# Router work laid along the slabs of the last attention projection, and memory's first steps behind the first experts

## The chip, the core and the metric

The kernel runs on one core of a Trainium2 chip. A core has engines with queues of their own: TensorE (PE in the profile, with its weight loads as PEld), VectorE (DVE), ScalarE (ACT), GpSimd (POOL) and SyncE (SP), which here issues the loads from HBM. Weights come into on-chip memory (SBUF) by DMA; products land in PSUM, in eight banks. The metric is the device time of one execution in microseconds (us), the median of several runs. Every fp32 weight is split into a high and a low part (h and l), and each product of a projection is three matmuls: h by xh, l by xh, h by xl.

## What is computed

A small decoder with two parts, for 256 tokens of width 1024, in fp32. Block 1 is attention and a mixture of 32 experts in four groups, with two experts for each token; behind it come two more layers (mixers, cross-attention into 256 memory tokens, a feed-forward part). Cut to what the change touches:

```python
x = x + mixed @ w_out[l]
x = x + hierarchical_moe(rmsnorm(x, ffn_norm[l]), ...)

def hierarchical_moe(h, ...):
    g_logits = hf @ w_rg + b_rg                # 4 groups
    g_sel = argmax(g_logits)
    p_group = softmax(g_logits)[g_sel]
    e_logits = einsum('td,gde->tge', hf, w_re) + b_re
    top_vals, top_idx = top_k(e_logits[g_sel], 2)
    weight = p_group * softmax(top_vals)
    ...
    ys = (silu(xb @ w_g[e]) * (xb @ w_u[e])) @ w_d[e]
    out = out.at[slot_tok].add(ys * slot_w)

def mem_attention(h, mem_n, ...):              # both later layers
    kv = (mem_n @ w_kv)                        # depends on mem alone
```

The keys and values of the memory depend on no token, so the kernel may compute them anywhere ahead of the later layers.

## The kernel before, in words

**Recording and planning.** The program is first recorded by `Recorder` (line 161) as a list of operations, then put in order by `plan` (line 290), a list scheduler with a price for each operation: each engine takes, of what is ready, the operation with the lowest place in the recording (`bias` shifts that place). It also hands out buffers. A tile has a tag; tiles of one tag take their slots in the order of recording. Loads are handed their slots strictly in that order too. A raw expert load (`raw`, line 542) has no tag: it takes a slot of whichever shared tag has most to spare, counting as taken those that tiles recorded ahead of it will still need (`spare`, line 309). Shared are `n8` (6 slots), `w`, `h` and `l` (3 each); each slot holds 1 MiB. The framework then fixes the final order of the single instructions on each engine, which may let one with a free slot pass another that waits.

**Slabs.** `slab` (line 548) loads 1 MiB of weights into `w`, ACT copies it into `h`, DVE subtracts into `l`. `fm` (line 672) multiplies a slab by all 256 tokens, channel by channel, into a PSUM bank of tag `g` (three banks).

**The last projection.** `block1_attention` (line 794) ends with one memory step (`prepare`, line 1325: load of the memory, its scaled parts and statistics) and `project` (line 711): four slabs of w_out, each followed by an add into x.

**The router.** `moe` (line 1046) then transposes x into the tiles hh and hl (16 transposes of 128 by 128), takes the squares of x (`sumsq`, line 653), and calls `route` (line 957): products with the router's weights `wr` as the stationary operand (36 columns, 256 tokens moving), a copy, two transposes back, some forty short DVE instructions that select groups and experts, a prefix count on PE (`pos`), and place. Two memory steps (`values`, line 1353) are recorded behind that with a lower priority (`MEM_EARLY`, `FILL`).

**The experts.** `gather` (line 1097) makes the selection matrix st for eight experts, picks their tokens by 32 matmuls, and makes each slot's norm factor and expert weight by matmuls of two scaled copies (rt, ct) with a column of ones (`rs`). Eight groups of four experts follow: `gate_up` (line 1142, eight raw loads of w_gu), `gated` (line 1154), `expert_out` (line 1168, four raw loads of w_dn). Between them stand memory steps, as many as `MEM_EVERY` says (line 36). Of 18 memory steps 16 are done by the end of the experts; the last two go into the following mixer.

Of the kernel before, what the change touches and what calls it, by code (L numbers as in the profile page):

```python
# [10 lines left out]
F32 = mybir.dt.float32  # L11
# [20 lines left out]
CUT = 2  # L32
MEM_EARLY = 2
FILL = 300
LATEG = 1
MEM_EVERY = (2, 2, 2, 2, 2, 2, 1, 0)

# [15 lines left out]
for _name, _width in (("ident", 128), ("cmask", 128), ("smask", 128), ("ulow", 128), ("ntri", 128),  # L53
                      ("bd64", 128), ("dist", 256), ("cm", 32), ("sm", 32), ("cb", 16), ("sb", 16),
                      ("slot", 32)):
    CST[_name] = (_off, _off + _width)
    _off += _width
# [104 lines left out]
class Recorder:  # L162
    LAG = 200.0
    shared = ("n8", "w", "h", "l")
    OWN = 70.0
# [306 lines left out]
class Net:  # L472
# [237 lines left out]

    def project(self, w, m):

        for s in range(4):
            b = self.fm(self.slab(w[s], 256), m)
            xs = self.x[:, 2 * s:2 * s + 2, :]
            self.rec.vector.tensor_tensor(xs, xs, self.two(b), ALU.add)


# [74 lines left out]

    def block1_attention(self, steps):
        nc, a = self.rec, self.a
# [127 lines left out]
        for n, wn in enumerate(("w_o_mla", "w_o_moba")):  # L923
            for s in range(2):
                w = self.slab(a[wn][s], 512)
                for q in range(2):
# [4 lines left out]
                    if n:  # L931
                        m = gates[0][:, c:c + 2, :]
                        nc.vector.tensor_tensor(m, m, gv, ALU.add)
                        self.parts(mx[0][:, c:c + 2, :], mx[1][:, c:c + 2, :], m)
        steps.pop(0)()
        self.project(a["w_out"], mx)

# [18 lines left out]

    def route(self, rtm):

        nc = self.rec
        tt, ts, red = nc.vector.tensor_tensor, nc.vector.tensor_scalar, nc.vector.tensor_reduce  # L960
        wr = self.temp("a", "wr", [128, KC, 36])
        tt(wr, self.par("wr").rearrange("p (k n) -> p k n", n=36),
           self.par("ffn_norm")[:, :, None].to_broadcast([128, KC, 36]), ALU.mult)
        b = self.bank("a", "rt")
        for k in range(KC):
            self.mm(b[0:36, :T], wr[:, k, :], self.x[:, k, :], k == 0, k == KC - 1)
        lt = self.temp("a", "lt", [128, T])
        nc.vector.tensor_copy(lt[0:36, :], b[0:36, :T])
        b = self.bank("a", "rt2")
        for t in range(2):  # L970
            nc.tensor.transpose(b[:, 64 * t:64 * t + 36], lt[0:36, 128 * t:128 * t + 128], self.ident[0:36, 0:36])
        board, used = self.temp("a", "route", [128, 400]), [0]

        def small(name, *s):
            if name in ("wt", "place", "wlate"):
                return self.small(name, 2, *s, bufs=1)
            o, used[0] = used[0], used[0] + 2 * int(np.prod(s))
            v = board[:, o:used[0]]
            return v.rearrange({0: "p t -> p t", 1: "p (t a) -> p t a", 2: "p (t a b) -> p t a b"}[len(s)],
                               **({"t": 2, "a": s[0]} if s else {}))  # L980
# [21 lines left out]
        tt(oa, o1, o2, ALU.add)  # L1002
        sel, wt = small("sel", 4, 8), small("wt", 4, 8)
        grouped = lambda out, v: [tt(out[:, t], v[:, t, None, :].to_broadcast([128, 4, 8]),
                                     g1[:, t, :, None].to_broadcast([128, 4, 8]), ALU.mult) for t in range(2)]
        grouped(sel, oa)
        sel, wtf = (q.rearrange("p t g e -> p t (g e)") for q in (sel, wt))
        selb = self.small("selb", 2, 32, dt=BF16, bufs=1)
# [34 lines left out]
        nc.vector.tensor_copy(flag[0:1, :], b[0:1, 0:1])  # L1043
        return wtf, place, wlate, flag

    def moe(self, steps, early, every):
# [3 lines left out]
        for q in range(2):  # L1050
            for t in range(2):
                b = self.bank("g", "xt")
                for j in range(4):
                    nc.tensor.transpose(b[:, 128 * j:128 * j + 128], x[:, 4 * q + j, 128 * t:128 * t + 128],
                                        self.ident)
                cs = slice(512 * q, 512 * q + 512)
                self.parts(hh[:, t, cs], hl[:, t, cs], b)
        rtm = self.rstd_by_token(self.sumsq(x))
        wt, place, wlate, flag = self.route(rtm)
        nc.bias = -FILL  # L1060
        for _ in range(early):
            steps.pop(0)()
        nc.bias = 0
        self.next = []
        xs, rest = self.gather(0, hh, hl, place, wt, rtm)
        banks = [self.bank("a", "gu")]
        self.gate_up(0, range(KC), xs, banks[0])
        for g in range(8):

            (st, rw), q = rest, g % 2  # L1070
# [8 lines left out]
            self.expert_out(g, 0, at, st, rw, q)  # L1079
            take = every[g]  # L1080
            if take:
                steps.pop(0)()
            if g < 7:
                self.gate_up(g + 1, range(KC // 2, KC), ahead, banks[g + 1])
            self.expert_out(g, 1, at, st, rw, q)
            if g % 2 == 0 and g < 6:
                ahead, later = self.gather(g // 2 + 1, hh, hl, place, wt, rtm)
            if q:
                xs = ahead
                if g < 7:  # L1090
                    rest = later
            if g == LATEG:
                nc.barrier(lambda: self.moe_late(hh, hl, rtm, wlate, flag), [hh, hl, rtm, wlate, flag, x])
            for _ in range(max(0, take - 1)):
                steps.pop(0)()

    def gather(self, p, hh, hl, place, wt, rtm):

        nc, slot = self.rec, self.c("slot")
        st = self.temp("a", "st", [128, 2, 8, SLOTS], F32R)  # L1100
        ct, rt = (self.temp("b", n, [128, 2, 8, SLOTS]) for n in ("ct", "rt"))
        for t in range(2):
            pe = lambda v: v[:, t, 8 * p:8 * p + 8][:, :, None].to_broadcast([128, 8, SLOTS])
            nc.vector.tensor_tensor(st[:, t], pe(place), slot[:, None, :].to_broadcast([128, 8, SLOTS]),
                                    ALU.is_equal)
            nc.vector.tensor_scalar(rt[:, t], st[:, t], rtm[:, t:t + 1], None, ALU.mult)
            nc.vector.tensor_tensor(ct[:, t], st[:, t], pe(wt), ALU.mult)
        stv, ctv, rtv = (v.rearrange("p t e s -> p t (e s)") for v in (st, ct, rt))
        xs = self.big("xs", [128, KC, 256])
        for i in range(4):  # L1110
# [6 lines left out]
            for j in range(2):  # L1117
                c = 2 * i + j
                gc = self.gcol("ffn_norm", c)
                if j:  # L1120
                    nc.scalar.activation(xs[:, c, :], b[:, 256 * j:256 * j + 256], AF.Copy, scale=gc)
                else:
                    nc.vector.tensor_scalar(xs[:, c, :], b[:, 256 * j:256 * j + 256], gc, None, ALU.mult)
        b = self.bank("m", "rs")
        for n, v in enumerate((rtv, ctv)):
            for i in range(2):
                for t in range(2):
                    self.mm(b[:, 2 * n + i:2 * n + i + 1], v[:, t, 128 * i:128 * i + 128], self.kone,
                            t == 0, t == 1)
        rw = self.small("rw", 4)  # L1130
        nc.vector.tensor_copy(rw, b[:, :4])

        b = self.bank("m", "sb")
        for i in range(2):
            for t in range(2):
                o = 256 * i + 128 * t
                nc.tensor.transpose(b[:, o:o + 128], stv[:, t, 128 * i:128 * i + 128].step("bitcast", F32), self.ident)
        sb = self.small("sb", 2, T, dt=F32R)
        nc.vector.tensor_copy(sb, self.two(b))
        return xs, (sb, rw)  # L1140

# [475 lines left out]
    def record(self, out):  # L1617
        steps = self.memory()
        self.block1_attention(steps)
        self.moe(steps, MEM_EARLY, MEM_EVERY)  # L1620
        x, rbc = self.two_norms()
# [94 lines left out]
def shape_constants():  # L1716
    c = np.zeros((128, NCST), np.float32)

    def put(name, v):
        s, e = CST[name]  # L1720
        c[:, s:e] = np.asarray(v, np.float32).reshape(128, e - s)
# [10 lines left out]
    for cn, sn, half in (("cm", "sm", 16), ("cb", "sb", 8)):  # L1732
# [3 lines left out]
        for n, fn in ((cn, np.cos), (sn, np.sin)):  # L1736
            put(n, fn(ang.astype(np.float64)).reshape(2, 128, half).transpose(1, 0, 2))
    put("slot", np.broadcast_to(np.arange(SLOTS) - 999.0, (128, SLOTS)))
    return c
# [16 lines left out]
```

## Time and profile before

| | us |
|---|---|
| median of 3 runs | 1278.55 |
| lowest and highest | 1278.52, 1281.36 |
| profiled execution, its own time | 1273.56 |
| its span, first to last instruction | 1271.8 |
| mean granted TensorE clock | 0.985 |

The busy shares on the page are means over the whole span; the two lines of digits below show how DMA traffic (GB/s) and PE move through it, in 40 slices of 31.8 us.

```profile
PE   7999999997889877997999999999999999999998
GB/s 274 237 100 133 205 249 210 323 411 356 420 419 419 419 383 290 186 147 100 169 163 67 216 194 184 172 197 172 160 133 133 118 165 100 182 197 173 185 177 64
```

Block 1's attention fills the first six slices, the router lies in the seventh, and the experts with most of the memory steps in slices 8 to 16.

### The profile page before, as it was taken

How to read it: one execution, taken by the hardware profiler on the slowest of the kernel's cores; microseconds unless marked ns; L12 is line 12 of the kernel's file. 1: busy time of each engine (PE TensorE's matmuls, PEld its weight loads, DVE VectorE, ACT ScalarE, POOL GpSimd, SP SyncE). 2: the span in 40 equal slices, each digit the busy share in tenths (PEclk: the TensorE clock that was granted, in tenths of full speed). 3: DMA queues.
4: the chain of work that ended last, by engine and by line, in shares of the span. 5: the costliest groups of instructions: out<-in, count | busy, mean ns of one | idle time of the engine just before them, and what ended most of it. 6: DMA issues, size and time to landing. Idle time of an engine off the chain costs nothing.

```text
span 1271.8 us, 22754 instructions
## 1 busy us (share of the span) xinstructions
PE 1213.5 (95%) x9371; PEld 1084.3 (85%) x9371; DVE 861.4 (68%) x1546; ACT 648.0 (51%) x1103; POOL 9.0 (1%) x70
## 2 busy tenths in 40 slices
PE   7999999997889877997999999999999999999998
PEld 7999999674555644997999999999999999999997
DVE  7666677424462345997787977777755687877775
ACT  7664554223332235555554655455766655555543
POOL 1000000000000000000000000000000000000000
PEclk9999999999899999998999999999999999999999
DMA  7623565898999997542541655555433342555551
GB/s 274 237 100 133 205 249 210 323 411 356 420 419 419 419 383 290 186 147 100 169 163 67 216 194 184 172 197 172 160 133 133 118 165 100 182 197 173 185 177 64
DMA packets 40141, 273.53 MB, mean 215 GB/s; under 512 B 4576, under 2 KB 4576, under 8 KB 8032
## 3 DMA queue, kind: packets, MB, share of 16 engines
q1 hardware_dynamic: 40032, 272.03, 57.2%
q8 instruction: 74, 1.21, 0.4%
q14 instruction: 35, 0.29, 0.1%
HBM read 270.96 MB, written 1.05 MB: 214 GB/s over the span
## 4 chain that ended last, share of the span: by engine, by line
PE 67%; DVE 5%; DMA 2%; ACT 1%; issue 0%; SPq 0%; ACTq 0%
PE fm L469 42%; PE dn L469 10%; PE tm L469 4%; PE gu L469 2%; PE oz L469 1%; DVE l L469 1%; PE mo L469 1%; PE ms L469 1%; DMA w<-w_gu 1%; PE by L469 1%; DMA w<-w_xkv 1%; PE hn L469 1%; DVE x L469 1%; PE bo L469 1%; PE st L469 1%; PE ga L469 0%
## 5 line engine op out<-in xcount | busy, mean ns | idle before, releaser
L469 PE MATMUL fm<-xh,h 128*128 128x256 f32 x1824 | 528.1, 290 | 17.1 <-ACT h L469 9.6
L469 PE MATMUL fm<-xh,l 128*128 128x256 f32 x1824 | 520.4, 286 | 5.8 <-DVE l L469 5.8
L469 PE MATMUL fm<-xl,h 128*128 128x256 f32 x1824 | 519.4, 285 | 0.0
L469 DVE TENSOR_TENSOR l<-w,h 128x1024 fp32r<-128x1024 f32 (+2 forms) x328 | 383.3, 1191 | 60.8 <-ACT h L469 60.0
L469 ACT ACTIVATE h<-w 128x1024 fp32r<-128x1024 f32 (+2 forms) x328 | 326.0, 1027 | 173.2 <-issue 84.3
L469 PEld LDWEIGHTS fm<-xh,h 128*128 128x128 f32 x1824 | 351.8, 193 | 26.3 <-ACT h L469 11.0
L469 PEld LDWEIGHTS fm<-xh,l 128*128 128x128 f32 x1824 | 352.0, 193 | 8.1 <-DVE l L469 7.5
L469 PEld LDWEIGHTS fm<-xl,h 128*128 128x128 f32 x1824 | 351.8, 193 | 6.0 <-issue 4.7
L469 PE MATMUL tm<-h,xh 128*128 128x256 f32 (+2 forms) x364 | 108.8, 300 | 0.9 <-DVE x L469 0.6
L469 PE MATMUL tm<-l,xh 128*128 128x256 f32 (+2 forms) x364 | 105.2, 290 | 3.1 <-DVE l L469 3.1
L469 PE MATMUL tm<-h,xl 128*128 128x256 f32 (+2 forms) x364 | 104.9, 289 | 0.0
L469 PEld LDWEIGHTS tm<-h,xh 128*128 128x128 f32 x364 | 70.5, 194 | 6.8 <-issue 3.6
L469 PEld LDWEIGHTS tm<-l,xh 128*128 128x128 f32 x364 | 70.6, 194 | 4.5 <-DVE l L469 3.7
L469 DVE SCALAR_TENSOR_TENSOR fc<-fu,partile,fc 128x256 f32<-128x256 f32 x176 | 73.5, 479 | 1.3 <-ACT fc L469 1.3
L469 PEld LDWEIGHTS tm<-h,xl 128*128 128x128 f32 x364 | 70.5, 194 | 2.8 <-issue 2.5
L469 PE MATMUL gu<-w,xs 128*32 128x512 f32 x512 | 67.3, 633 | 0.2 <-PEq L1206 0.2
L469 PE MATMUL dn<-fa,h 128*128 128x256 f32 x352 | 64.2, 282 | 1.1 <-ACT fa L469 0.6
L469 PE MATMUL dn<-h,fa 128*128 128x512 f32 x176 | 57.0, 396 | 0.0
L469 DVE TENSOR_TENSOR fu<-fm,rbc 128x512 f32<-128x512 f32 x44 | 30.3, 688 | 37.9 <-PE fm L469 37.7
L469 PEld LDWEIGHTS dn<-fa,h 128*128 128x128 f32 x352 | 54.4, 189 | 1.6 <-ACT fa L469 0.8
L469 DVE SCALAR_TENSOR_TENSOR yl<-by,rw,yh 128x512 fp32r<-128x512 f32 x16 | 12.0, 749 | 55.7 <-ACT yh L469 55.7
L469 PE MATMUL dn<-fa,l 128*128 128x256 f32 x176 | 49.6, 282 | 0.0
(276 smaller groups left out, 1375.2 us busy)
## 6 DMA issues: line engine op xcount, KB each, us to landing
w<-w_gu SPq DMA_DIRECT2D x64, 1024.0 KB, 10.9
w<-w_up SPq DMA_DIRECT2D x44, 1024.0 KB, 4.9
w<-w_dn SPq DMA_DIRECT2D x32, 1024.0 KB, 12.4
w<-w_down SPq DMA_DIRECT2D x22, 1024.0 KB, 4.9
w<-w_xkv SPq DMA_DIRECT2D x16, 1024.0 KB, 9.2
w<-w_in_d SPq DMA_DIRECT2D x8, 1024.0 KB, 4.8
w<-w_xq SPq DMA_DIRECT2D x8, 1024.0 KB, 4.9
w<-w_xo SPq DMA_DIRECT2D x8, 1024.0 KB, 4.9
```

Of the source, the lines that this page charges most:

```text
L469: self.last[engine.engine] = getattr(engine, method)(*map(r, a), **{n: r(v) for n, v in k.items()})
```

## The change

Each slab of w_out is followed at once by its share of what the router needs. `project` gets a function `after` that runs behind each slab's add: two chunks of x times `wr` for both halves of the tokens (x is now the stationary operand, so the logits come out by token and the copy and the two transposes back are gone), the squares of the two chunks, and behind every second slab the transposes and the split into hh and hl.

No memory step is recorded ahead of the experts any more: `prepare` leaves `block1_attention`, `MEM_EARLY` and `FILL` are gone, and `MEM_EVERY` is larger (16 steps instead of 13), the first three of them at the end of group 0. The tags `xh` and `xl` join the shared ones, each with two slots.

`gather` is split. The part that picks tokens stays; the factors are made in `scatter`, recorded for the first pair of groups behind `gate_up(0)`: the transposed selection times one matrix `factors` of 33 columns (the norm factor and 32 expert weights), of which each slot takes its own column with a constant mask `own`.

```diff
-MEM_EARLY = 2
-FILL = 300
-MEM_EVERY = (2, 2, 2, 2, 2, 2, 1, 0)
+MEM_EVERY = (3, 2, 2, 3, 2, 2, 2, 0)
...
-    shared = ("n8", "w", "h", "l")
+    shared = ("n8", "w", "h", "l", "xh", "xl")
...
-    def project(self, w, m):
+    def project(self, w, m, after=None):
...
             self.rec.vector.tensor_tensor(xs, xs, self.two(b), ALU.add)
+            if after:
+                after(s)
...
-        steps.pop(0)()
-        self.project(a["w_out"], mx)
+        return mx
...
-        for k in range(KC):
-            self.mm(b[0:36, :T], wr[:, k, :], self.x[:, k, :], k == 0, k == KC - 1)
-        lt = self.temp("a", "lt", [128, T])
-        nc.vector.tensor_copy(lt[0:36, :], b[0:36, :T])
-        b = self.bank("a", "rt2")
-        for t in range(2):
-            nc.tensor.transpose(b[:, 64 * t:64 * t + 36], lt[0:36, 128 * t:128 * t + 128], self.ident[0:36, 0:36])
...
+        def prepared(s):
+
+            for k in (2 * s, 2 * s + 1):
+                for t in range(2):
+                    self.mm(logits[:, 64 * t:64 * t + 36], x[:, k, 128 * t:128 * t + 128], wr[:, k, :],
+                            k == 0 and t == 0, k == KC - 1)
+            self.squares(self.pair(x, s), acc, s == 0)
+            if s % 2:
+                q = s // 2
+                for t in range(2):
+                    b = self.bank("g", "xt")
+                    for j in range(4):
+                        nc.tensor.transpose(b[:, 128 * j:128 * j + 128], x[:, 4 * q + j, 128 * t:128 * t + 128],
+                                            self.ident)
+                    cs = slice(512 * q, 512 * q + 512)
+                    self.parts(hh[:, t, cs], hl[:, t, cs], b)
+
+        self.project(a["w_out"], mx, prepared)
+        rtm = self.rstd_by_token(acc)
+        factors, place, wlate, flag = self.route(rtm, logits)
...
-        rtm = self.rstd_by_token(self.sumsq(x))
-        wt, place, wlate, flag = self.route(rtm)
-        nc.bias = -FILL
-        for _ in range(early):
-            steps.pop(0)()
-        nc.bias = 0
...
+        xs, st = self.gather(0, hh, hl, place)
         banks = [self.bank("a", "gu")]
         self.gate_up(0, range(KC), xs, banks[0])
+        rest = self.scatter(0, st, factors)
...
-            if take:
+            if g and take:
                 steps.pop(0)()
...
-            for _ in range(max(0, take - 1)):
+            for _ in range(take if g == 0 else max(0, take - 1)):
...
-            nc.vector.tensor_scalar(rt[:, t], st[:, t], rtm[:, t:t + 1], None, ALU.mult)
-            nc.vector.tensor_tensor(ct[:, t], st[:, t], pe(wt), ALU.mult)
...
+    def scatter(self, p, stv, factors):
+        one = lambda t, i: stv[:, t, 128 * i:128 * i + 128].step("bitcast", F32)
+        b = self.bank("m", "rs")
+        for i in range(2):
+            for t in range(2):
+                self.mm(b[:, 64 * i:64 * i + 33], one(t, i), factors[:, t, :], t == 0, t == 1)
+        bv = b[:, :128].rearrange("p (i n) -> p i n", i=2)
...
+        nc.vector.tensor_copy(rw[:, 0:2], bv[:, :, 0])
+        nc.vector.tensor_tensor(own, bv[:, :, 1 + 8 * p:9 + 8 * p],
+                                self.c("own").rearrange("p (i e) -> p i e", i=2), ALU.mult)
+        nc.vector.tensor_reduce(rw[:, 2:4], own, axis=AX.X, op=ALU.add)
```

More of the change, by code (lines that the diff above doesn't have):

```diff
@@ L54 @@
                       ("bd64", 128), ("dist", 256), ("cm", 32), ("sm", 32), ("cb", 16), ("sb", 16),
-                      ("slot", 32)):
+                      ("slot", 32), ("own", 16)):
     CST[_name] = (_off, _off + _width)
@@ L791, in rope, with block1_attention @@
         tt(x2, ts[2], ts[3], ALU.add)
-    def block1_attention(self, steps):
+    def block1_attention(self):
         nc, a = self.rec, self.a
@@ L955, in first_of, with route @@
         nc.vector.tensor_tensor(out, order, m[:, :, None].to_broadcast(shape), ALU.is_equal)
-    def route(self, rtm):
+    def route(self, rtm, b):
         nc = self.rec
         tt, ts, red = nc.vector.tensor_tensor, nc.vector.tensor_scalar, nc.vector.tensor_reduce
[L961 to L964, printed above, removed]
-        for k in range(KC):
-            self.mm(b[0:36, :T], wr[:, k, :], self.x[:, k, :], k == 0, k == KC - 1)
-        lt = self.temp("a", "lt", [128, T])
-        nc.vector.tensor_copy(lt[0:36, :], b[0:36, :T])
-        b = self.bank("a", "rt2")
-        for t in range(2):
-            nc.tensor.transpose(b[:, 64 * t:64 * t + 36], lt[0:36, 128 * t:128 * t + 128], self.ident[0:36, 0:36])
         board, used = self.temp("a", "route", [128, 400]), [0]
         def small(name, *s):
-            if name in ("wt", "place", "wlate"):
+            if name in ("place", "wlate"):
                 return self.small(name, 2, *s, bufs=1)
@@ L1002, in route @@
         tt(oa, o1, o2, ALU.add)
-        sel, wt = small("sel", 4, 8), small("wt", 4, 8)
+        sel = small("sel", 4, 8)
+        factors = self.small("factors", 2, 33, bufs=1)
+        nc.vector.tensor_copy(factors[:, :, 0], rtm)
+        wtf = factors[:, :, 1:33]
+        wt = wtf.rearrange("p t (g e) -> p t g e", g=4)
         grouped = lambda out, v: [tt(out[:, t], v[:, t, None, :].to_broadcast([128, 4, 8]),
@@ L1006, in route @@
         grouped(sel, oa)
-        sel, wtf = (q.rearrange("p t g e -> p t (g e)") for q in (sel, wt))
+        sel = sel.rearrange("p t g e -> p t (g e)")
         selb = self.small("selb", 2, 32, dt=BF16, bufs=1)
@@ L1043, in route, with moe @@
         nc.vector.tensor_copy(flag[0:1, :], b[0:1, 0:1])
-        return wtf, place, wlate, flag
-    def moe(self, steps, early, every):
+        return factors, place, wlate, flag
+    def moe(self, steps, every, mx):
         nc, a, x = self.rec, self.a, self.x
         hh, hl = (t.rearrange("p (t q) n -> p t (q n)", t=2) for t in self.xtiles())
[L1050 to L1057, printed above, removed]
-        rtm = self.rstd_by_token(self.sumsq(x))
-        wt, place, wlate, flag = self.route(rtm)
-        nc.bias = -FILL
-        for _ in range(early):
-            steps.pop(0)()
-        nc.bias = 0
+        acc = self.tile([128, 512], "acc", "acc", 2)
+        wr = self.temp("a", "wr", [128, KC, 36])
+        nc.vector.tensor_tensor(wr, self.par("wr").rearrange("p (k n) -> p k n", n=36),
+                                self.par("ffn_norm")[:, :, None].to_broadcast([128, KC, 36]), ALU.mult)
+        logits = self.bank("a", "rt")
+        def prepared(s):
[16 more added lines that the diff above has]
+        factors, place, wlate, flag = self.route(rtm, logits)
@@ L1064, in moe @@
         self.next = []
-        xs, rest = self.gather(0, hh, hl, place, wt, rtm)
+        xs, st = self.gather(0, hh, hl, place)
         banks = [self.bank("a", "gu")]
         self.gate_up(0, range(KC), xs, banks[0])
+        rest = self.scatter(0, st, factors)
         for g in range(8):
-            (st, rw), q = rest, g % 2
+            (sb, rw), q = rest, g % 2
             at = self.gated(banks[g], rw, q)
@@ L1078, in moe @@
                 self.next.append(self.slab(a["w_eqk"][0], 256))
-            self.expert_out(g, 0, at, st, rw, q)
+            self.expert_out(g, 0, at, sb, rw, q)
             take = every[g]
-            if take:
+            if g and take:
                 steps.pop(0)()
@@ L1084, in moe @@
                 self.gate_up(g + 1, range(KC // 2, KC), ahead, banks[g + 1])
-            self.expert_out(g, 1, at, st, rw, q)
+            self.expert_out(g, 1, at, sb, rw, q)
             if g % 2 == 0 and g < 6:
-                ahead, later = self.gather(g // 2 + 1, hh, hl, place, wt, rtm)
+                ahead, st = self.gather(g // 2 + 1, hh, hl, place)
+                later = self.scatter(g // 2 + 1, st, factors)
             if q:
@@ L1093, in moe, with gather @@
                 nc.barrier(lambda: self.moe_late(hh, hl, rtm, wlate, flag), [hh, hl, rtm, wlate, flag, x])
-            for _ in range(max(0, take - 1)):
+            for _ in range(take if g == 0 else max(0, take - 1)):
                 steps.pop(0)()
-    def gather(self, p, hh, hl, place, wt, rtm):
+    def gather(self, p, hh, hl, place):
         nc, slot = self.rec, self.c("slot")
         st = self.temp("a", "st", [128, 2, 8, SLOTS], F32R)
-        ct, rt = (self.temp("b", n, [128, 2, 8, SLOTS]) for n in ("ct", "rt"))
         for t in range(2):
-            pe = lambda v: v[:, t, 8 * p:8 * p + 8][:, :, None].to_broadcast([128, 8, SLOTS])
-            nc.vector.tensor_tensor(st[:, t], pe(place), slot[:, None, :].to_broadcast([128, 8, SLOTS]),
-                                    ALU.is_equal)
-            nc.vector.tensor_scalar(rt[:, t], st[:, t], rtm[:, t:t + 1], None, ALU.mult)
-            nc.vector.tensor_tensor(ct[:, t], st[:, t], pe(wt), ALU.mult)
-        stv, ctv, rtv = (v.rearrange("p t e s -> p t (e s)") for v in (st, ct, rt))
+            pe = place[:, t, 8 * p:8 * p + 8][:, :, None].to_broadcast([128, 8, SLOTS])
+            nc.vector.tensor_tensor(st[:, t], pe, slot[:, None, :].to_broadcast([128, 8, SLOTS]), ALU.is_equal)
+        stv = st.rearrange("p t e s -> p t (e s)")
         xs = self.big("xs", [128, KC, 256])
@@ L1123, in gather @@
                     nc.vector.tensor_scalar(xs[:, c, :], b[:, 256 * j:256 * j + 256], gc, None, ALU.mult)
+        return xs, stv
+    def scatter(self, p, stv, factors):
+        nc = self.rec
+        one = lambda t, i: stv[:, t, 128 * i:128 * i + 128].step("bitcast", F32)
         b = self.bank("m", "rs")
[L1125 to L1129, printed above, removed]
-        rw = self.small("rw", 4)
-        nc.vector.tensor_copy(rw, b[:, :4])
+        for i in range(2):
+            for t in range(2):
+                self.mm(b[:, 64 * i:64 * i + 33], one(t, i), factors[:, t, :], t == 0, t == 1)
+        bv = b[:, :128].rearrange("p (i n) -> p i n", i=2)
+        rw = self.small("rw", 4)
+        own = self.small("own", 2, 8, bufs=1)
+        nc.vector.tensor_copy(rw[:, 0:2], bv[:, :, 0])
+        nc.vector.tensor_tensor(own, bv[:, :, 1 + 8 * p:9 + 8 * p],
+                                self.c("own").rearrange("p (i e) -> p i e", i=2), ALU.mult)
+        nc.vector.tensor_reduce(rw[:, 2:4], own, axis=AX.X, op=ALU.add)
         b = self.bank("m", "sb")
@@ L1136, in gather @@
                 o = 256 * i + 128 * t
-                nc.tensor.transpose(b[:, o:o + 128], stv[:, t, 128 * i:128 * i + 128].step("bitcast", F32), self.ident)
+                nc.tensor.transpose(b[:, o:o + 128], one(t, i), self.ident)
         sb = self.small("sb", 2, T, dt=F32R)
         nc.vector.tensor_copy(sb, self.two(b))
-        return xs, (sb, rw)
+        return sb, rw
     def gate_up(self, g, ks, xs, bg):
@@ L1618, in record @@
         steps = self.memory()
-        self.block1_attention(steps)
-        self.moe(steps, MEM_EARLY, MEM_EVERY)
+        self.moe(steps, MEM_EVERY, self.block1_attention())
         x, rbc = self.two_norms()
@@ L1737, in shape_constants @@
             put(n, fn(ang.astype(np.float64)).reshape(2, 128, half).transpose(1, 0, 2))
+    put("own", np.arange(8)[None, None, :] == 4 * np.arange(2)[None, :, None] + r[:, :, None] // 32)
     put("slot", np.broadcast_to(np.arange(SLOTS) - 999.0, (128, SLOTS)))
```

## The prediction

> **What bounds the kernel now.** I read the page first, then a table of stages, then who waits for whom, then the order of the loads, then the router's instructions one by one.
>
> ```profile
> span 1271.8 us, 22754 instructions
> PE 1213.5 (95%) x9371; PEld 1084.3 (85%) x9371; DVE 861.4 (68%) x1546; ACT 648.0 (51%) x1103; POOL 9.0 (1%) x70
> DMA  7623565898999997542541655555433342555551
> ```
>
> PE is busy 95% of the span, but the fourth line of digits shows one stretch where DMA is full. The table by stage (PE, PEld, DVE, ACT, POOL busy, granted clock, DMA share, GB/s) separates them:
>
> ```profile
> 170.00:232.00 62.00, 62.00 (x498) 58.83 (x497) 47.57 (x112) 29.18 (x46) 0.00 (x0) 1.00 0.55 200
> 232.00:505.00 273.00, 234.28 (x1719) 146.00 (x1719) 111.62 (x203) 86.61 (x126) 0.00 (x0) 0.94 0.96 394
> 236.00:300.00 64.00, 57.84 (x437) 36.52 (x437) 19.83 (x33) 13.66 (x20) 0.00 (x0) 0.92 0.99 399
> 300.00:320.00 20.00, 15.76 (x121) 8.39 (x120) 8.79 (x15) 7.26 (x9) 0.00 (x0) 1.00 0.80 320
> 320.00:470.00 150.00, 129.37 (x944) 80.42 (x943) 61.97 (x117) 46.43 (x70) 0.00 (x0) 0.94 1.01 419
> 470.00:505.00 35.00, 27.31 (x186) 16.67 (x187) 19.43 (x35) 16.85 (x23) 0.00 (x0) 0.95 0.78 314
> 560.00:1271.00 711.00, 699.12 (x5419) 672.70 (x5417) 535.14 (x886) 394.95 (x666) 5.15 (x48) 1.00 0.44 156
> ```
>
> From 170 to 232 (last projection, router, two memory slabs) PE never rests and DMA is 45% idle. From 232 to 505 (the experts) it is the reverse: DMA is at 0.96 and PE idles 273 - 234.3 = 38.7 us. At 419 GB/s a load of 1 MiB takes 1.0486 MB / 419 GB/s = 2.50 us. Behind 505 PE is full again, and the diff changes nothing there. So the change is to be judged by a ledger of loads: how many of them are done before the experts, and how many are left for the stage that DMA bounds.
>
> ```profile
> 145.71 0.42 SPq L469 DMA_DIRECT2D mem<-mem  x1
> 151.47 0.42 SPq L469 DMA_DIRECT2D w<-w_gu  x1
> 162.94 0.42 SPq L469 DMA_DIRECT2D w<-w_gu  x1
> 168.32 11.89 SPq L469 DMA_DIRECT2D w<-w_out  x3
> 187.45 9.06 SPq L469 DMA_DIRECT2D w<-w_xkv  x2
> 199.72 31.48 SPq L469 DMA_DIRECT2D w<-w_gu  x9
> 475.63 6.71 SPq L469 DMA_DIRECT2D w<-w_dn  x4
> SPq L469 <- PE gu L469: 78.0, 44, 8.7
> SPq L469 <- DVE l L469: 63.3, 10, 8.9
> PE co L469 <- ACT yh L469: 9.7, 12, 0.9
> PE fm L469 <- DVE l L469: 5.8, 3, 1.9
> ```
>
> These are SP's loads up to the experts, their last four, and the longest waits of SP and two of PE within 232 to 505 (us in total, times, longest). SP issues in order and waits for a free slot: memory input and two w_xkv slabs go ahead of most of w_gu. Three w_gu went early (151, 157, 163), nine between 199.7 and 231.2.
>
> **The change part by part.**
>
> *Loads.* A raw expert load may sit in any spare n8, w, h or l slot (6+3+3+3), now also xh and xl. Before, by 232: 62 us x 200 GB/s = 12.4 MB = 11.8 MiB, of which some 2.7 are w_out and 2 w_xkv; so 7 w_gu, with the three early ones 10. After, no memory step stands ahead of the first 20 expert loads. Spare are n8 less one kept for xs (5), w, h and l as w_out's slabs are used up (9), and one xh and one xl when mx is done: 16. The last six of these (two h/l pairs and xh, xl) come free in the last 10 us of the projection, early enough to land before the router ends. So 6 more expert loads are in. Against that 3 loads (mem, two w_xkv) move behind, onto SP's queue after the 20 loads of the first two groups. Net 3 loads x 2.50 = **-7.5 us**. Should only 13 be in, the net is 0; with all 16 in and two losses of the before (the 20% missing in 300 to 320, 4 us) gone, it is -11.5.
>
> *When the first expert starts.*
>
> ```profile
> 187.79 0.59 PE L469 MATMUL st<-acc,ones 128*128 128x256 f32 x2
> 212.11 0.69 DVE L469 TENSOR_TENSOR x<-x,fm 128x512 f32<-128x512 f32 x1 [1.78 <-PE fm L469]
> 213.04 0.62 ACT L469 ACTIVATE sq<-x 128x512 f32<-128x512 f32 x1
> 213.78 0.68 DVE L469 TENSOR_TENSOR acc<-acc,sq 128x512 f32<-128x512 f32 x1
> 214.98 0.42 DVE L469 TENSOR_TENSOR acc<-acc 128x256 f32<-128x256 f32 x1
> 217.65 0.50 PE L469 MATMUL st<-ones,acc 128*128 128x1 f32 x4
> 218.01 0.36 PE L469 MATMUL tm<-h,xh 128*128 128x256 f32 x1
> 220.03 0.42 DVE L469 SCALAR_TENSOR_TENSOR route<-rt,rtm,partile 128x36 f32<-128x36 f32 x2
> 225.16 0.19 DVE L469 CAST selb<-route 128x64 bf16<-128x64 f32 x1
> 228.16 0.23 DVE L469 SCALAR_TENSOR_TENSOR place<-pos,route 128x64 f32<-128x64 f32 x1 [2.11 <-PE pos L469]
> 230.41 0.39 PE L469 MATMUL ga<-st,xh 128*128 128x256 f32 x1
> 234.35 0.95 PE L469 MATMUL rs<-order,rt 128*128 128x1 f32 x8
> 236.12 1.07 PE L469 MATMUL gu<-w,xs 128*32 128x512 f32 x8
> L469 PE MATMUL rt<-x,wr 128*36 128x256 f32 x16 | 3.8, 382 | 0.0
> L469 PE MATMUL xt<-csttile,x 128*128 128x128 f32 x16 | 2.3, 279 | 0.0
> ```
>
> The new logits have x as the 128-wide stationary operand, which no row shows with 36 columns. Nearest is rs, 128-wide with one column: eight records in 0.95 us, 0.12 each, two to a product. Sixteen products are then 32 x 0.12 = 3.8 us, just what rt costs; at rt's own 0.24 a record it would be 7.6. I take 3.8, 0.95 a slab. The transposes are the same 2.3 us. PE is full up to 212, so three slabs' logits (2.9) and the first half of the transposes (1.1) push the last projection back by 4 us; memory's statistics (0.6) leave. The xt banks now take turns with fm's three banks, so a slab can wait for the add of the one before: up to 1.2 us (add 0.69 and its handshakes); I take 1. The last fm product ends at 212.1 - 0.6 + 4 + 1 = 216.5. Behind it stand the add 0.7, the square 0.6 (as other squares of 512 on ACT), the acc add 0.7, its fold 0.4, st 0.3 and the 2.4 that passed from 217.65 to 220.03: the logits with bias at about 221.5, **+1.5**. The squares were off the path before, since PE held st up with rt; now they are on it.
>
> From there to selb 5.1 us, as before. Then DVE sat idle for 2.11 us, because pos stood behind memory's products in PE's order. PE is empty now; with 0.4 for pos, place comes at 227.0 (-1.2). From place to the gather were 2.25 us, with rt and ct between the two halves of st; they are gone, so 1.1: gather at 228.1 (-2.3). PE has then idled some 9 us, and a row shows what that costs:
>
> ```profile
> 251.52 1.95 PE L469 MATMUL rs<-order,rt 128*128 128x1 f32 x8 [1.95 <-DVE rt L469]
> 257.53 0.41 PE L469 MATMUL tm<-h,xh 128*128 128x256 f32 x1
> 257.74 0.41 PE L469 MATMUL tm<-l,xh 128*128 128x256 f32 x1
> 250.00:260.00 10.00, 8.35 (x42) 7.32 (x43) 5.62 (x10) 2.22 (x3) 0.00 (x0) 0.66 1.02 422
> ```
>
> Behind the gap of 1.95 us products still start 0.21 us apart six microseconds later, and the granted clock of the window is 0.66. The gather's 32 products took 3.9 us (230.41 to 234.35, 0.12 apart); at 0.21 they take 6.9, **+3.0**. The Trainium skill, "TensorE: Matmul & The Clock Gate", Part 1, says that an idle window of some 3.4 us halves the clock and that as long a busy one restores it. By that rule the gather would lose about 1.7 us only, and the sum below would be 1.3 better; the slow spell from 251.5 to beyond 257.7 is longer than the rule, so the row stands.
>
> The gather ends at 235.0, and gu follows at once, since rs (1.8 us) is now recorded behind it: first expert at 235.1 against 236.12, **-1.0**. DMA stands still until the first w_gu slot is released, a good microsecond later, where before it ran already: **+0.5**.
>
> *PE work moved into the experts.* Two value slabs (PE filled 218.0 to the gather's 230.4 with them: 12.4 us) and memory's statistics go into the stage; rs shrinks from 16 records to 8 in four gathers, 0.95 x 4 = 3.8 us less; DVE loses rt and ct and gets a few small instructions instead. PE has 38.7 us idle there. To end 8 us sooner with 9 us more work it must run with about 22 idle. Its waits for casts (such as fm for l) are waits for DMA and may go; those in the experts' own chain (co for yh, twelve of 0.8) must partly be filled by the added slabs. That is tight, so I put **+1.0** (0 to 4) for DMA running dry now and then because PE releases late. Memory's 16 pieces and squares on ACT and DVE move too; both are under half busy in the stage, so nothing is charged.
>
> Sum: -7.5 - 1.0 + 0.5 + 1.0 = **-7.0 us**. The profiled execution took 1273.56 us (span 1271.8 and 1.8 around it), hence 1266.5; the median of the timed runs, 1278.55, lies 5 above it, and I forecast from that: **1271.5**.
>
> **Rivals.**
> - *Fewer loads come early.* A slot freed late, or one assigned to a load that comes too late, leaves 12 or 13 in instead of 16: 3 or 4 x 2.5 takes 7.5 to 10 away, 1279 to 1281.5; half of that, 1275 to 1276. For it: the nine of before came in bursts. Against it: three slots were used over 70 us ahead.
> - *PE becomes the bound of the experts* (the other side). If the 38.7 us idle are the chain's own, the moved work adds its full length: routing leaves 9 us of PE bare, the cold clock 3.0, less 3.8 for rs: +8.2, 1286.8. It decides from the point where PE's idle time in the stage can't fall below about 30 us. For it: PE's waits name ACT and DVE more than casts. Against it: DMA at 1.01 for 150 us, with SP's next load waiting.
> - *The dips go too*: the ledger's -11.5 in place of -7.5, and no charge of 1.0 for running dry: -12, 1266.5.
>
> **How the numbers follow.** Forecast (gain 4 to 10) 0.52, dips gone 0.11, fewer loads 0.24, PE bound 0.13. Only differences over 0.3%, 3.8 us, can be told from no change. Faster 0.64 (the first two and a little of the third), same 0.24, slower 0.12. The range runs from the third rival, widened by 1.5 (half of the gather's +3.0, should the clock recover sooner), to fewer loads at their worst: 1265 to 1281.5.
>
> **What would show it.** The changed profile should have some 16 expert loads issued before the first gu, PE idle 8 to 10 us between st and the gather at a low clock, gu starting at 234 to 236, DMA at or over 0.96 from there, and the last w_dn issue 7 to 9 us earlier than its 482 (475.63 + 6.71). PE's idle time in the stage should fall to 20 to 25 us. It is wrong if DMA's share in the stage falls under 0.93 (then PE bounds), if gu starts behind 238, or if only a dozen w_gu are issued before it.

## The result and the profile after

The changed kernel takes 1294.2 us, the median of 4 runs (1292.59 to 1294.46); the kernel before took 1278.89 beside it. The ratio is 1.012, with a 95% interval of 1.0098 to 1.0142: slower by 15 us, where 7 less were forecast, and outside the range.

The profiled execution of the changed kernel took 1294.46 us, at the upper end of its runs, and that of the kernel before 1273.56, 5 below its median. So the spans differ by 20.9 us where the medians differ by 15.3; 5 to 6 of what follows belong to the two executions and not to the change. First the page: span, busy times and the DMA digits, each for 32.3 us.

```profile
span 1292.7 us, 22705 instructions
PE 1216.1 (94%) x9353; PEld 1087.0 (84%) x9353; DVE 857.4 (66%) x1538; ACT 644.8 (50%) x1101; POOL 7.4 (1%) x70
DMA  7633568789969997443251554554443252555551
```

PE's busy time is nearly the same (1216.1 against 1213.5), so the 20.9 us are mostly idle time of PE. The DMA line has a dip (a 6) in the middle of the stretch that was full before. The table by stage (busy us of PE, PEld, DVE, ACT, POOL, granted clock, DMA share, GB/s) of the changed kernel: router, experts (first gu to last co), all behind them, and two stretches of the experts.

```profile
180.00:236.00 56.00, 45.87 (x369) 44.65 (x367) 33.58 (x86) 18.42 (x28) 0.00 (x0) 0.91 0.66 251
236.00:522.90 286.90, 242.05 (x1752) 152.09 (x1752) 118.26 (x215) 92.76 (x142) 0.00 (x0) 0.91 0.89 363
522.90:1292.70 769.80, 755.03 (x5860) 725.50 (x5858) 588.38 (x997) 428.72 (x728) 5.04 (x48) 1.00 0.44 155
320.00:470.00 150.00, 128.87 (x928) 83.24 (x920) 62.92 (x117) 46.55 (x70) 0.00 (x0) 0.93 0.92 378
350.00:370.00 20.00, 17.08 (x104) 14.62 (x108) 5.71 (x16) 1.74 (x4) 0.00 (x0) 0.75 0.44 183
```

The same row of the kernel before, for its experts:

```profile
236.10:505.00 268.90, 230.18 (x1683) 141.90 (x1684) 110.02 (x199) 84.20 (x121) 0.00 (x0) 0.94 0.96 393
```

The experts begin at the same time (236.0 and 236.1) and end 17.9 later: 286.9 us instead of 268.9. PE idles 286.9 - 242.05 = 44.8 there, where it idled 38.7 before, and another 56.0 - 45.87 = 10.1 in the router, where it idled nothing. Idle time is 10.1 + 6.1 + 1.7 (behind the experts) more, with 0.3 ahead of 180, and busy time 2.6: that makes up the 20.9 but for rounding. DMA fell from 0.96 to 0.89 of the stage, that is from about 11 idle us (268.9 x 0.04) to 32.

The loads explain the dip. SP's loads in the changed kernel (start, us, count), the four early ones by the first and the last:

```profile
148.24 0.42 SPq L467 DMA_DIRECT2D w<-w_gu  x1
...
165.47 0.42 SPq L467 DMA_DIRECT2D w<-w_gu  x1
173.88 8.87 SPq L467 DMA_DIRECT2D w<-w_out  x3
189.98 21.72 SPq L467 DMA_DIRECT2D w<-w_gu  x8
217.53 0.80 SPq L467 DMA_DIRECT2D w<-w_dn  x2
218.39 19.96 SPq L467 DMA_DIRECT2D w<-w_gu  x4
...
350.32 21.40 SPq L467 DMA_DIRECT2D w<-w_gu  x4
...
487.03 10.99 SPq L467 DMA_DIRECT2D w<-w_dn  x4
```

By the landing times 16 expert loads were in at 236, against 10 before. But the four w_gu from 350.3 take 21.4 us to issue, and the last w_dn is issued at 487.03 + 10.99 = 498.0, 16 later than before, not 7 to 9 earlier. What SP waited for between 350 and 372, in the view of waits (total, times, longest):

```profile
SPq L467 <- PE fm L467: 18.8, 1, 18.8
```

SP stood 18.8 us at one load, because its slot was held by a memory slab that PE had not yet multiplied. PE came to that slab at 363.6: until 351.57 it had waited 4.5 us for DVE's selection matrix (`ga <- DVE st` in the list of PE's waits further down), and the gather, its products at first 0.21 us apart, went ahead of the slab. DMA waited for PE here; in the stretch from 350 to 370 it moved 183 GB/s instead of 419.

### The profile page after: what moved, and what is told of

Its sections match the earlier page's. It is cut to its first block, busy times and chain, and to the rows that moved or that the text cites. A ratio compares the mean times of both kernels' runs of the same rounds, so it can differ in the third digit from the quotient of the medians.

```text
span 1292.7 us, 22705 instructions
## 1 busy us (share of the span) xinstructions
PE 1216.1 (94%) x9353; PEld 1087.0 (84%) x9353; DVE 857.4 (66%) x1538; ACT 644.8 (50%) x1101; POOL 7.4 (1%) x70
## 4 chain that ended last, share of the span: by engine, by line
PE 68%; DVE 5%; ACT 2%; issue 1%; DVEq 0%; ACTq 0%
PE fm L467 42%; PE dn L467 10%; PE tm L467 5%; PE gu L467 3%; DVE l L467 1%; PE oz L467 1%; PE by L467 1%; PE mo L467 1%; PE ms L467 1%; PE hn L467 1%; PE bo L467 1%; PE co L467 1%; DVE x L467 1%; PE ga L467 1%; DVE rsq_t L467 1%
## 5 line engine op out<-in xcount | busy, mean ns | idle before, releaser
L467 ACT ACTIVATE fc<-fc 128x256 f32<-128x256 f32 x44 | 18.4, 418 | 56.3 <-DVE fc L467 56.3
```

The source lines that it names most:

```text
L467: self.last[engine.engine] = getattr(engine, method)(*map(r, a), **{n: r(v) for n, v in k.items()})
```

## The experiments

Where a stage is given, "experts" is the time from the first gu to the last co in the profile, "idle" PE's idle time in it. Ratios are against the kernel before, run beside each experiment (its own median there was between 1276.1 and 1279.22), so kernels of different groups are compared by their ratios.

**One half at a time.** `e1` keeps the new router and the split gather, and puts memory's steps and the shared tags back as they were (`prepare` ahead of the last projection, two slabs behind the route, 13 steps in the experts, of which one is the second `prepare` and 12 are slabs). From the changed kernel:

```diff
-MEM_EVERY = (3, 2, 2, 3, 2, 2, 2, 0)
+MEM_EVERY = (2, 2, 2, 2, 2, 2, 1, 0)
...
-    shared = ("n8", "w", "h", "l", "xh", "xl")
+    shared = ("n8", "w", "h", "l")
...
+        steps.pop(0)()
         self.project(a["w_out"], mx, prepared)
...
         factors, place, wlate, flag = self.route(rtm, logits)
+        nc.bias = -300
+        for _ in range(2):
+            steps.pop(0)()
+        nc.bias = 0
...
-            if g and take:
+            if take:
...
-            for _ in range(take if g == 0 else max(0, take - 1)):
+            for _ in range(max(0, take - 1)):
```

> The changed kernel with the memory steps where they were (the first ahead of the last projection, two behind the router at low priority, 2 2 2 2 2 2 1 0 behind), xh and xl not shared: the router's part of the change alone. Theory A (the loss of 15 us comes from memory's first steps standing among the first experts, where their long ACT and DVE work holds the in-order queues and lets DMA run dry): 1274 to 1280, since only 3.8 us of rs products and the copies go and the last projection is 4 us longer. Theory B (the loss comes from the router part: squares on the path, logits in the way of the projection): 1285 to 1294.

`e2` does the opposite in the kernel before: no step ahead of the experts, `MEM_EVERY` and shared tags of the changed kernel, the old router.

```diff
-MEM_EVERY = (2, 2, 2, 2, 2, 2, 1, 0)
+MEM_EVERY = (3, 2, 2, 3, 2, 2, 2, 0)
...
-    shared = ("n8", "w", "h", "l")
+    shared = ("n8", "w", "h", "l", "xh", "xl")
...
-        steps.pop(0)()
         self.project(a["w_out"], mx)
...
-        nc.bias = -FILL
-        for _ in range(early):
-            steps.pop(0)()
-        nc.bias = 0
...
-            if take:
+            if g and take:
...
-            for _ in range(max(0, take - 1)):
+            for _ in range(take if g == 0 else max(0, take - 1)):
```

> The kernel before with the new placement of the memory steps (none ahead of the experts, 3 2 2 3 2 2 2 0) and with xh and xl shared, but with the old router and gather. Theory A: 1288 to 1298, the loss is all there. Theory B: 1272 to 1280. If the router stage of 9 idle us on PE is the loss (theory C), 1286 to 1292, with DMA's share in the experts unchanged at 0.96.

| kernel | median us | ratio (95%) | experts | idle | loads in |
|---|---|---|---|---|---|
| before | 1278.89 | 1 | 268.9 | 38.7 | 10 |
| after | 1294.2 | 1.012 (1.0098 to 1.0142) | 286.9 | 44.8 | 16 |
| `e1` router alone | 1270.17 | 0.9952 (0.9932 to 0.9971) | 268.4 | 36.2 | 10 |
| `e2` memory alone | 1297.11 | 1.017 (1.0128 to 1.0213) | 287.0 | 40.2 | 16 |

The whole loss lies in memory's steps: `e2` alone loses as much as the change, as theory A expected, and `e1` alone gains 0.5%, more than either theory gave it. `e1` beats both kernels and is the version to keep. The stage rows of `e1` (router, experts) against those above:

```profile
180.00:237.10 57.10, 55.31 (x461) 54.10 (x459) 41.56 (x105) 26.75 (x45) 0.00 (x0) 1.00 0.55 199
237.10:505.50 268.40, 232.25 (x1667) 138.91 (x1667) 107.28 (x196) 84.69 (x123) 0.00 (x0) 0.93 0.96 394
```

With the two slabs behind the route PE idles 57.10 - 55.31 = 1.8 us in the router instead of 10.1, at a clock of 1.00. The span of `e1`'s profiled execution is only 1.0 below that of before, against 7 in the medians, so no profile here says where its gain comes from.

**Two parts of the memory half.** `e3` is the changed kernel with the old shared tags; `e4` has memory's `prepare` back ahead of the last projection, and one step less in group 0.

```diff
-    shared = ("n8", "w", "h", "l", "xh", "xl")
+    shared = ("n8", "w", "h", "l")
```

> The changed kernel with only n8, w, h and l shared, as before. Theory A: 1291 to 1298, two slots fewer for loads ahead of the experts, up to 5 us. Theory D (raw expert loads that take xh or xl slots hold up memory's own xh and xl, and with them the in-order queues): 1278 to 1286, the holes in DMA near 270 and 350 smaller.

```diff
-MEM_EVERY = (3, 2, 2, 3, 2, 2, 2, 0)
+MEM_EVERY = (2, 2, 2, 3, 2, 2, 2, 0)
...
+        steps.pop(0)()
         self.project(a["w_out"], mx, prepared)
```

> The changed kernel with memory's first step (load, scaled parts, statistics) ahead of the last projection as before, the two value slabs and the rest as changed (2 2 2 3 2 2 2 0). Theory A in its narrow form (the first step is what holds DVE and ACT from 264 to 280): 1284 to 1289, the hole of DMA at 270 to 280 gone, that at 350 to 370 left. If any two or three slabs in the first group do it: 1291 to 1296.

`e3` took 1289.54 us (1.0113, 1.0068 to 1.0157) and `e4` 1295.11 (1.0146, 1.0103 to 1.0189). With 14 and 13 loads in, their experts took 283.7 and 285.7 us: neither the shared xh and xl nor `prepare` is the cause. `e3` lies between its two ranges, and its interval overlaps that of the changed kernel (1.0098 to 1.0142), so no cost of sharing is shown.

DMA's dip from 350 to 370 is not the loss either. Under theory A `e4` was to keep it, and it does not have it:

```profile
350.00:370.00 20.00, 18.90 (x142) 13.93 (x140) 9.55 (x20) 6.00 (x10) 0.00 (x0) 0.91 0.96 374
```

Its experts are nearly as long all the same, 285.7 us against 286.9.

**Less DMA, or less PE.** If the loads bound the experts, fewer of them must shorten the stage by 2.5 us each; if PE does, lighter memory slabs must. `x1` (the changed kernel) and `x2` (the one before) load only every second w_dn slab and multiply by it twice, 16 loads fewer. In both:

```diff
-            w = self.raw(self.a["w_dn"][g, 2 * k + i])
+            if k == 0:
+                w = self.raw(self.a["w_dn"][g, 2 * k + i])
```

> The changed kernel, but each pair of w_dn loads is one load whose weights serve both products (so half of the experts' down projection uses the wrong weights): 16 MiB less to load in the experts, 40 us of DMA at 2.5 us each, with the same instructions on PE, ACT and DVE. If DMA bounds the changed kernel's experts: 1255 to 1270. If PE with its own waits bounds them: 1286 to 1294.

> The same cut of 16 MiB in the kernel before. If DMA bounds its experts, as the prediction took from a DMA share of 0.96: 1245 to 1262, the 38.7 us of PE idle there falling to some 15. If PE with its own waits bounds them and full DMA is only what the free slots allow: 1270 to 1278, PE's idle time still over 30.

`m1` (the changed kernel) and `m2` (the one before) make one product of three for memory's keys and values, the high parts alone, and leave the other two out; `light` is set in the steps `values` and `keys` and nowhere else.

```diff
+            if self.light:
+                calls.append(("matmul", (out, sh, mh), dict(k, start=start, stop=stop)))
+                continue
```

> The same in the changed kernel, 14 slabs among the experts and 2 behind. If PE bounds: 1228 to 1240, as far above the kernel before with the same cut as the changed kernel was above it. If DMA's floor holds both, the changed kernel gets back what it lost, since with less PE work the loads that are in early count: 1238 to 1256, within 5 us of the other or below it.

> The kernel before with one product instead of three for each of the 16 memory slabs (high part by high part alone, so keys and values are less exact): 4.1 us of PE less per slab, 12 of them among the experts (50 us), 4 elsewhere (16 us), all loads and casts as they were. If PE's own work and waits bound the experts: 1212 to 1225. If DMA's rate is a floor for them (98 loads of 2.50 us, 245 of the 269 us they take): they can lose 10 to 20 us only, 1240 to 1255.

Medians: `x1` 1270.17 (0.9932, 0.9908 to 0.9957), `x2` 1264.99 (0.9901, 0.9876 to 0.9925), `m1` 1264.86 (0.9917, 0.9887 to 0.9947), `m2` 1264.08 (0.9905, 0.9873 to 0.9937). Their rows of the experts, `x1`:

```profile
236.40:497.30 260.90, 234.57 (x1770) 149.30 (x1770) 120.73 (x215) 94.91 (x145) 0.00 (x0) 0.96 0.85 340
```

`x2`:

```profile
235.90:490.70 254.80, 221.84 (x1664) 136.88 (x1665) 107.09 (x192) 81.17 (x116) 0.00 (x0) 0.95 0.87 349
```

`m1`:

```profile
236.70:499.50 262.80, 199.56 (x1314) 103.22 (x1314) 120.64 (x219) 94.49 (x142) 0.00 (x0) 0.86 0.96 396
```

`m2`:

```profile
235.80:496.50 260.70, 202.45 (x1299) 97.64 (x1300) 110.82 (x199) 84.74 (x121) 0.00 (x0) 0.85 0.98 403
```

Both theories in their pure form fall. Taking 16 loads (40 us of DMA) from the kernel before shortens its experts by 14.1 us, 0.9 a load and not 2.5. Taking 27.7 us of PE's busy time shortens them by 8.2. (The 384 products left out are worth 46 us at the 0.12 us that a product takes at the full clock; busy time falls by less because the granted clock falls too, from 0.94 to 0.85.) In the changed kernel the same edits give 26.0 for the loads, 1.6 a load, and 24.1 for 42.5 us of PE. What is left when PE is relieved is the same in both, 260.7 and 262.8: that is near DMA's limit (at 419 GB/s the bytes moved in these stages would take 251 and 248 us), and `m2`'s waits of PE now name it:

```profile
PE by L469 <- DMA w<-w_dn: 15.7, 17, 1.5
PE gu L469 <- DMA w<-w_gu: 8.4, 7, 1.8
```

The kernel before stood 8 us above that limit, the changed one 24. So before, the two limits lay close together, and a DMA share of 0.96 with SP always at a taken slot was the look of both of them. Of the ranges only a part of `m1`'s was met: it came within 5 us of `m2`, but both kernels stayed some 9 us above the upper end that a floor by DMA gave them, `x2` fell between its two ranges, and `x1` reached the upper end of the one for DMA.

**How the length follows the slabs.** The next four separate the number of memory slabs in the experts from the loads that are in at their start. `x3` is the changed kernel with the old `MEM_EVERY` (three slabs fewer in the experts, done behind them instead).

```diff
-MEM_EVERY = (3, 2, 2, 3, 2, 2, 2, 0)
+MEM_EVERY = (2, 2, 2, 2, 2, 2, 1, 0)
```

> The changed kernel with the old 2 2 2 2 2 2 1 0: three memory slabs (18.6 us of PE, 7.5 us of DMA) leave the experts for the mixer behind, where PE is full. If PE bounds the experts: 1290 to 1298, the slabs cost the same in both places. If DMA bounds them: 1300 to 1307. If the crowding in groups 0 and 3 is the loss: 1276 to 1286.

`x4` and `z1` are `e1` with one and with three early slabs, the other ones moved to or from group 0; `z2` is `e1` with none and the others behind the experts, so that the router's wait stays bare.

```diff
-MEM_EVERY = (2, 2, 2, 2, 2, 2, 1, 0)
+MEM_EVERY = (3, 2, 2, 2, 2, 2, 1, 0)
...
-        for _ in range(2):
+        for _ in range(1):
```

> The router's part alone (the first experiment of this kind), with one value slab instead of two behind the router and one more in the first group. One slab fills 6 of the 10 us in which PE waits for the router. If what counts is PE's bare time there and nothing is won back among the experts: 1274 to 1280. If a slab in the first group costs more than its own 6 us: 1282 to 1290. If the ledger of loads holds: 1264 to 1269.

```diff
-MEM_EVERY = (2, 2, 2, 2, 2, 2, 1, 0)
+MEM_EVERY = (1, 2, 2, 2, 2, 2, 1, 0)
...
-        for _ in range(2):
+        for _ in range(3):
```

> The router's part alone with three value slabs behind the router instead of two and one fewer in the first group. If PE's idle time among the experts can't be filled by slabs, a slab costs the same 6 us in front as behind: 1268 to 1273. If experts are bound by DMA, a slab less there saves 2.5 and one more in front costs 6: 1273 to 1277. If the first group is where slabs hurt, 1262 to 1267.

```diff
-        nc.bias = -300
-        for _ in range(2):
-            steps.pop(0)()
-        nc.bias = 0
```

> The router's part alone, but the two value slabs that filled the router's wait are not recorded there and the later steps are left as they were in number: the experts keep 12 slabs, the mixer behind gets two more. Only the wait is bare. If a bare wait costs its own length (10 us of PE less what PE idled before, some 8) and the experts stay as they are: 1277 to 1282. If the experts get worse too although they hold no more work: 1284 to 1292. If a bare wait is won back because loads run ahead in it: 1268 to 1273.

| kernel | median us | ratio (95%) | slabs that PE ran in the experts | loads in | experts | idle |
|---|---|---|---|---|---|---|
| `x3` | 1288.15 | 1.0083 (1.0064 to 1.0102) | 11 | 16 | 266.2 | 42.0 |
| `z1` | 1276.61 | 0.9979 (0.9965 to 0.9992) | nearly 12 (11 recorded) | 8 | 268.6 | 39.0 |
| `e1` | 1270.17 | 0.9952 (0.9932 to 0.9971) | 12 | 10 | 268.4 | 36.2 |
| `z2` | 1294.2 | 1.0124 (1.0093 to 1.0155) | 12 | 13 | 268.0 | 40.8 |
| `x4` | 1278.08 | 0.9995 (0.9983 to 1.0008) | 13 | 12 | 273.4 | 38.0 |
| `e3` | 1289.54 | 1.0113 (1.0068 to 1.0157) | 14 | 14 | 283.7 | 39.4 |
| `e4` | 1295.11 | 1.0146 (1.0103 to 1.0189) | 14 | 13 | 285.7 | 40.9 |
| after | 1294.2 | 1.012 (1.0098 to 1.0142) | 14 | 16 | 286.9 | 44.8 |

The rows behind it for the pair that decides, `z2` (router, experts, all behind):

```profile
180.00:237.70 57.70, 46.77 (x366) 45.14 (x364) 37.39 (x101) 21.39 (x38) 0.00 (x0) 0.88 0.54 201
237.70:505.70 268.00, 227.16 (x1663) 136.04 (x1663) 101.04 (x180) 76.27 (x115) 0.00 (x0) 0.94 0.95 388
505.70:1289.80 784.10, 767.45 (x5944) 737.80 (x5943) 598.29 (x1013) 434.81 (x738) 4.99 (x48) 0.99 0.45 155
```

and `x3`'s experts:

```profile
234.60:500.80 266.20, 224.21 (x1621) 132.15 (x1621) 106.04 (x197) 86.67 (x131) 0.00 (x0) 0.91 0.94 379
```

`z1` needs a count of its own. These are the products of the value slabs (tile tm, 48 to a slab) among its experts, and below them those among `e1`'s:

```profile
243.20:511.80 268.60, 40.81 (x280) 0.94 0.97 401
237.10:505.50 268.40, 40.59 (x288) 0.93 0.96 394
```

By the recording `z1` should have 240 there. PE ran only 8 of the third slab's 48 products ahead of the first gu and the other 40 in the experts.

The loads in at the start are worth next to nothing: with 12 slabs, 8, 10 and 13 of them give 268.6, 268.4 and 268.0 us, and with 14 slabs, 13, 14 and 16 give 285.7, 283.7 and 286.9. The slabs count: 11 and 12 take 265 to 269 us, the 13th adds 5, the 14th another 10 to 15 (the two by-ways below are counted in: `y4` with 12 slabs takes 264.9, `y3` with 14 takes 288.7). With 11 and with 13 slabs there is one kernel each, so these steps are rough. Idle time stays at 36 to 45 in all of them, so what the added slabs bring is mostly their own busy time (230.2 us in the experts of the kernel before, 242.1 in the changed one). Number and place are not separated: the added slabs stand in groups 0, 3 and 6, and no run puts them elsewhere.

Beyond these 12, a slab finds free room in one place only, the router's wait. `z2` has `e1`'s experts, but the two slabs run behind them, where PE is full: 784.1 us instead of 1270.8 - 505.5 = 765.3, and by the ratios it takes some 22 us more. That is above all of its ranges. One slab in the wait instead of two costs some 5.5 by the ratios (`x4`, as its first range had it), at most its own PE time. What a third slab in the wait costs `z1` doesn't show, since that slab mostly ran elsewhere; its experts start 6 later (243.2 against 237.1), with the first two slabs beginning at 224.9 instead of 220.7, and by the ratios it takes some 3.5 more than `e1`. `x3` lies between its ranges.

**Two by-ways.** `y4` is `e1` with xh and xl shared.

```diff
-    shared = ("n8", "w", "h", "l")
+    shared = ("n8", "w", "h", "l", "xh", "xl")
```

> The router's part alone, with xh and xl shared for raw loads as in the change. Without the memory steps in the experts' first groups few of these slots are ever spare: 1268 to 1273. If sharing itself disturbs the order (theory D, for which the run without it gave 4.7 us): 1274 to 1279.

It took 1271.72 (0.9943, 0.9922 to 0.9964); the interval overlaps `e1`'s almost wholly, so no gain or loss is seen. `y3` doubles the distance at which the changed kernel hints at instructions beyond a branch:

```diff
-    AHEAD = 120
+    AHEAD = 240
```

> The changed kernel with the branch hint placed 240 planned operations ahead of the branch instead of 120. In the changed kernel's trace PE's branch took 6.14 us against 0.39 in the kernel before, with all engines held. If the hint came too late: 1287 to 1290, PE's branch at 0.4. If its distance doesn't matter: 1292 to 1296.

It took 1293.75 (1.0108, 1.0069 to 1.0146): no effect is seen. What it was for stands in the last section.

## Why the prediction was wrong

**The ledger's entries were right, its worth was not.** 16 expert loads came early, as forecast, and three loads moved behind them. The step took it for granted that DMA alone bounds the experts, so that a load less is 2.5 us less. The runs price a load in this stage at 0.9 us in the kernel before (`x2`) and 1.6 in the changed one (`x1`), and a load that is only earlier at about nothing (`z2` against `e1`, and the kernels with 14 slabs).

**The step that failed** is "PE work moved into the experts": with the added slabs PE's idle time was to fall from 38.7 to about 22. It rose to 44.8, and with the two slabs (12.4 us of PE) the stage became 18 us longer: 12 of busy time and 6 of idle time. The "+1.0 (0 to 4) for DMA running dry because PE releases late" is where this should have appeared: DMA idled some 21 us more. It is the second rival's mechanism, PE as the bound of the experts, with its condition met (idle can't fall below 30), and the prediction's own sign for it, a DMA share under 0.93. That rival got 0.13; the prediction's argument against it, DMA at 1.01 with SP waiting, carried too much weight, since a queue that waits for slots is also what a late PE leaves. Its price (+8.2) was too low as well, by about 7 in the medians: it took the bare wait for 9 us and let the experts only keep pace. Measured are 10.1 for the wait, 6.1 more idle time in the experts and 1.7 behind them. The range ended at 1281.5, below the 1286.8 of this rival, so it left out a case that had been given a chance. Why the idle time grows with the added slabs instead of being filled is not settled. The longest waits of PE in the stage don't name one culprit:

```profile
PE at L467 <- DVE act L467: 8.4, 3, 7.9
PE co L467 <- ACT yh L467: 7.6, 8, 1.9
PE tm L467 <- DVE l L467: 5.0, 4, 1.7
PE ga L467 <- DVE st L467: 4.5, 1, 4.5
PE fm L467 <- DVE l L467: 4.4, 3, 1.9
```

Some are the experts' own chain (co, ga), some casts of slabs that came late (tm, fm), and the 7.9 at `at` stands behind the branch of the last section.

**When the first expert starts** was nearly right, 236.0 against 235.1, partly by luck: the logits came 2.0 later than forecast, and the gather lost 1.1 less. The router in the trace of the changed kernel (start, duration, what it waited for):

```profile
212.26 0.98 PE L467 MATMUL rt<-wr,x 128*128 128x36 f32 x8
217.66 0.69 DVE L467 TENSOR_TENSOR x<-x,fm 128x512 f32<-128x512 f32 x1 [4.56 <-PE fm L467]
223.50 0.26 DVE L467 SCALAR_TENSOR_TENSOR route<-rt,rtm,partile 128x36 f32<-128x36 f32 x1
228.93 0.18 PE L467 MATMUL pos<-selb,bf 128*128 128x32 bf16 x1 [6.85 <-DVE selb L467]
229.21 0.23 DVE L467 SCALAR_TENSOR_TENSOR place<-pos,route 128x64 f32<-128x64 f32 x1
230.24 0.55 PE L467 MATMUL ga<-st,xh 128*128 128x256 f32 x1 [1.07 <-DVE nlate L467]
...
233.36 0.41 PE L467 MATMUL ga<-st,xh 128*128 128x256 f32 x1
233.57 0.41 PE L467 MATMUL ga<-st,xl 128*128 128x256 f32 x1
...
235.24 0.28 PE L467 MATMUL ga<-st,xh 128*128 128x256 f32 x1
235.35 0.28 PE L467 MATMUL ga<-st,xl 128*128 128x256 f32 x1
236.03 2.35 PE L467 MATMUL gu<-w,xs 128*32 128x512 f32 x20
```

- The logits cost 0.98 a slab (forecast 0.95). The projection's last product ended at 217.6 (forecast 216.5), and logits and bias came at 223.5 (221.5).
- From there to place were 5.7 us (forecast 5.5), to the gather 1.0 (1.1).
- Behind PE's wait of 6.85 the gather's products start 0.21 apart until about 233.8 and 0.12 apart behind it: 5.8 us instead of 3.9, **+1.9** where +3.0 was charged. The Trainium skill, "TensorE: Matmul & The Clock Gate", Part 1, gives 3.4 us of busy time until the full clock is back, from which the prediction's estimate of 1.7 lost came. The measurement (3.6 us at the slow spacing) agrees with it. The row that the prediction preferred does show a longer spell, the granted clock at 0.50 from about 251.7 to 258.5 with PE busy, but it begins with the one-column products of rs; from its first 256-column product, at 255.04, it too lasts 3.5 us. Whether one-column products count as busy time, no run here tests.
- The +0.5 for DMA's start can't be checked: DMA stood nearly still from 230 to 236 (4 GB/s and less), as all early loads had landed, and no run separates what that costs.

So the small terms held or cancelled, and the sign was lost in the one large term, the ledger's -7.5, and in the premise under it that the experts had idle PE time to spare.

## What to carry to other kernels

A DMA queue at 0.96 that always waits for a slot doesn't show that loads bound a stage: loads and compute that share slots look so when both limits lie close together, so price a load and a product by taking some away before work is moved from one to the other. A wait that already has filling (here 12.4 us of slabs in a wait of 10) is the cheapest place in the kernel for it; move it out only into a stage whose idle time has been shown to take work. Where a change has two halves, run each alone: here one gains 0.5% and the other loses 1.7%.

## What was not expected of the hardware

PE's conditional branch around the rare late tokens cost 0.39 us in the kernel before and 6.1 in the changed one. PE's sequencer there, before (duration in ns, times):

```profile
L1206 PEldq COMPARE_BRANCH  x1: 392/392/392, 308.9 to 308.9; - x1
```

after:

```profile
L1217 PEldq COMPARE_BRANCH  x1: 6139/6139/6139, 307.2 to 307.2; - x1
```

`y3`, with the hint given twice as far ahead:

```profile
L1217 PEldq COMPARE_BRANCH  x1: 6024/6024/6024, 307.0 to 307.0; - x1
```

Behind it stands PE's longest wait in the experts, 7.9 us at `at`. The branch took 3.8 us in `e3` and 6.0 in `x1`, but 0.4 in the eleven other experiments. It does not explain the loss: `e2` and `e4` have the short branch and experts of 287.0 and 285.7 us. Its cause stays open; doubling the distance of the hint did not change it.
